# A hybrid decoder layer on one core: low-weight products last in each tile, columns normalised ahead of the input projection, a three-operation step in the top-k search

## The chip, the cores and the metric

The kernel runs on one core of a Trainium2 chip. The metric is the device time of one execution in microseconds. All times of the kernel before come from three runs and from one more execution that the hardware profiler recorded.

## The reference

One decoder layer for 1040 positions (16 meta tokens and 1024 of input) of 1024 channels:

```python
h = rms_norm(stream, mix_norm_g)
proj = h @ w_in          # conv branch, q/k/v, indexer q/k/weights, two gates
q, k, q_idx, k_idx = rope(...)
y_a = silu(layer_norm(conv31(a * sigmoid(gate)))) @ conv_pw_out
score = sum_h w_idx[h] * relu(q_idx[h] . k_idx)       # causal, meta keys first
keys  = top_k(score, 256)                             # per query
y_b = softmax(q . k[keys]) @ v[keys] @ attn_w_o
stream += (sigmoid(g_a) * y_a + sigmoid(g_b) * y_b) @ w_merge_out
h = rms_norm(stream, ffn_norm_g)
stream += (silu(a) * b) @ ffn_down                    # a, b = conv3(h @ ffn_up)
out = rms_norm(stream, final_norm_g)
```

`rms_norm` scales each position by the inverse root of its mean square, and each channel by a gain.

## The kernel before, in words

**Layout.** Channels lie on the 128 partitions and positions along the free axis, so an activation is eight tiles (`k` = 0 to 7) of 1044 columns. Column work is cut into three chunks of 348 (`CW`) or, without the first columns, of 342 (`QW`).

**Matrix products.** Every product is made of three in a 32-bit form that TensorE rounds: each operand is split into a high half (a rounded copy) and a low half (the rest). `mm` (L176) computes one tile of 128 output rows: for each `k` in turn it issues high weight by high data, high weight by low data, and low weight by high data, each for up to three chunks of columns. With eight `k` and three chunks that is 72 matmuls, each with its own weight load, into three banks of PSUM. `psm` (L203) alternates between two sets of three banks.

**Weights.** `wload` (L110) brings weight tile `i`: SP loads `wr`, ScalarE copies it to the high half `wh` (L117), writes its negative to `wl` (L121), and POOL issues a transfer that adds the weights from DRAM to it (L122), so that `wl` becomes the low half. The first two tiles take a VectorE subtraction instead (L119). There are three buffers of `wh` and two of `wl` and of `wr`; `wget` asks for a tile and the two behind it.

**The opening.** The input tiles `x` arrive chunk by chunk. Each is multiplied by its gain on the way into the high half `hh` (ScalarE, L274) and the low half `hl` (VectorE, L275). The squares (L284, L286) are added on POOL, or in the last chunk on VectorE (L288), summed over partitions by TensorE (`stat_mm`, L239, a column of ones as moving operand), turned into the inverse root `r` (`rstd_small`, L241), and spread over all partitions by TensorE (`bcast_mm`, L254) into `rx` (L295). The factor of the position comes in later, at each place where a projection is used: in the rope tables (L304), the values (through `rpos`, L335 and L340, which TensorE transposes from `rx`, L391), the indexer weights (L395), the convolution branch (L660 before its tanh and L673 on POOL), and the gates.

**Input projection.** The loop at L645 goes over units in a fixed list: convolution channel tiles, indexer keys and queries, gates, q, k and v. A gate tile is copied out of PSUM (L696) and stored to DRAM; `load_gate` (L762) fetches it during the projections `w_pw` and `w_o`, multiplies it by `rx` on POOL (L766) and takes its tanh on ScalarE (L767). Beside the units, `background` steps through the depthwise convolution taps (VectorE, L580) and the search for the top-k threshold.

**The search** (`topk_search`, L486) finds, for each query, the bits of the threshold from the highest down, for two groups of query blocks. For a bit ScalarE counts the scores at or above a candidate (L483). VectorE prepares the two candidates of the next bit (L503, L504), and behind the count compares (L507) and copies under the comparison to the next candidate (L509) and to `key` (L510).

**Behind it** come the projection `w_pw` (L796), attention over eight heads, the output projection `w_o`, the merge `w_merge`, and the feed-forward part in five groups (`w_up`, `w_down`).

**Order of work.** The program is written in this order, and a planner in the framework lays out each engine's own instruction list from it by simulated times and priorities; work under `urgent()` is moved ahead. On the chip every engine works through its list in order and waits on semaphores. SP and POOL issue transfers in the order of their lists too.

Of the kernel before, what the change touches and what calls it, by code (L numbers as in the profile page):

```python
# [11 lines left out]
F32 = mybir.dt.float32  # L12
# [65 lines left out]
def body(ctx: ExitStack, tc: tile.TileContext, xT, vecs, w_idx, w_v, w_conv, w_k, w_q, w_gate,  # L78
# [97 lines left out]
    def mm(ps, w, rh, rl, nk, cols, woff=0):  # L176
        wh, wl = w
        for k in range(nk):
            sl = slice(woff + k * P, woff + (k + 1) * P)
            for pi, (ww, rr) in enumerate(((wh, rh), (wh, rl), (wl, rh))):  # L180
                for ci, (c0, n) in enumerate(cols):
                    pe.matmul(ps[:, ci, :n], lhsT=ww[:, sl], rhs=rr[k][:, c0:c0 + n],  # L182
                              start=(k == 0 and pi == 0), stop=(k == nk - 1 and pi == 2))
# [49 lines left out]
    def vcol(i):  # L233
        return vec[:, i:i + 1]
# [25 lines left out]

# [5 lines left out]
    rx = ft("rx")  # L266
    rpos = base.tile([P, NB + 1], F32, name="rpos")
# [3 lines left out]
    for c in range(NCH):  # L271
        cs = slice(c * CW, (c + 1) * CW)
        for k in range(KT):
            act.activation(hh[k][:, cs], xs[k][:, cs], AF.Copy, scale=vcol(V_MG + k))  # L274
            dve.scalar_tensor_tensor(hl[k][:, cs], xs[k][:, cs], vcol(V_MG + k), f(hh[k])[:, cs], op0=ALU.mult,  # L275
                                     op1=ALU.subtract)
    acc = tmp("acc")
    for c in range(NCH):
        cs = slice(c * CW, (c + 1) * CW)
        for k in range(KT):  # L280
            sq = tmp(f"sq{c}_{k}") if k else None
            dst = sq[:, :CW] if k else acc[:, cs]
            if k % 2 and c < NCH - 1:
                dve.tensor_tensor(dst, xs[k][:, cs], xs[k][:, cs], op=ALU.mult)  # L284
            else:
                act.activation(dst, xs[k][:, cs], AF.Square)  # L286
# [3 lines left out]
    with urgent():  # L290
        r = rstd_small(PS[:, 6, :], BW, 9, "n1")
        for c in range(NCH):
            sb = bank("s", (7, 6))
            bcast_mm(sb, r, BW, 3 * c, 3)
            act.copy(rx[:, c * CW:(c + 1) * CW], sb[:, :CW])  # L295
    del xs
    d_rx = dram.tile([P, LQ], F32, name="drx")
# [15 lines left out]
    def values(ws):  # L313
# [10 lines left out]
        for b in range(NB + 1):  # L324
# [8 lines left out]
            with urgent():  # L333
                if b == 0:
                    act.activation(vm, ps[:M0, :VW], AF.Copy, scale=rpos[:M0, 0:1])  # L335
                else:
# [3 lines left out]
                    act.activation(vf[:, q * VW:(q + 1) * VW], ps[:, :VW], AF.Copy, scale=rpos[:, b:b + 1])  # L340
# [28 lines left out]
    def index_keys(w):  # L369
# [18 lines left out]
        sp_ = bank("s", (6, 7))  # L388
        for b in range(NB + 1):
            c0, m = (0, M0) if b == 0 else (M0 + P * (b - 1), P)  # L390
            pe.transpose(sp_[:m, b:b + 1], rx[0:1, c0:c0 + m], ident[:1, :1])  # L391
        act.copy(rpos[:M0, 0:1], sp_[:M0, 0:1])
        act.copy(rpos[:, 1:], sp_[:, 1:NB + 1])
        wqv = wq.rearrange("p j h -> p (j h)")[:, IH:]
        dve.scalar_tensor_tensor(wq[:, 1:, :], sb[:, IH:NB * IH].rearrange("p (j h) -> p j h", h=IH), IH ** -0.5,  # L395
                                 rpos[:, 2:].rearrange("p (j o) -> p j o", o=1).to_broadcast([P, NB - 1, IH]),
                                 op0=ALU.mult, op1=ALU.mult)
# [88 lines left out]
    def topk_search():  # L486
# [687 lines left out]
```

## Time and profile before

| | us |
|---|---|
| median of three runs | 1903.15 |
| lowest, highest | 1901.66, 1908.85 |
| the profiled execution | 1905.48 |
| its span, first to last instruction | 1903.7 |

The profiled execution lies 2.3 us above the median, and 1.8 us of it lie around its span. Its mean granted TensorE clock is 0.985 of full speed. Engines in the rows: PE is TensorE's matmuls, PEld its weight loads, DVE is VectorE, ACT ScalarE, POOL GpSimd, SP the engine that issues plain transfers; a `q` behind a name means its queue. A row names the line, the engine, the operation, the tile written and the tiles read; `<-` behind a time names what ended the wait. TensorE's matmuls overlap, so the mean of one is longer than the step from one to the next.

### The profile page before, as it was taken

To read this page: it belongs to the slowest core of one execution; us is meant where nothing else is said; L and a number is where in the kernel's file an instruction comes from. 1 tells how busy PE (TensorE), PEld (TensorE's weight loads), DVE (VectorE), ACT (ScalarE), POOL (GpSimd) and SP (SyncE) were. 2 spreads that over 40 slices of the span, in tenths; PEclk is the share of its full clock that TensorE was granted. 3 is DMA by queue.
4 is the path that set the end of the run, shared out by engine and by line. 5 is a ranking of instruction groups with operands and counts; after the bars stand their busy time and mean duration, and the time that the engine had idled before them with its cause. 6 is when DMAs were issued, how large, how long until landed. Compare 5 with 4: busy or idle time off the path is not lost.

```text
span 1903.7 us, 27576 instructions
## 1 busy us (share of the span) xinstructions
PE 1826.9 (96%) x11131; PEld 1755.1 (92%) x11131; DVE 1025.3 (54%) x1582; ACT 985.4 (52%) x1568; POOL 463.2 (24%) x395
## 2 busy tenths in 40 slices
PE   8889899999999989999999999999999999999997
PEld 7879799999999989899999999988998999899987
DVE  6597598998954392588833223331432233133436
ACT  6555477888799933688732334322332233233325
POOL 4533332122123235122221221111121111111122
PEclk9999999999999999999999999999999999999999
DMA  5533467777656588421267444444434443544342
GB/s 183 125 78 86 99 139 165 157 167 155 144 133 156 128 194 221 101 68 46 78 177 199 89 111 89 85 87 105 95 78 93 102 90 78 119 90 89 67 91 97
DMA packets 71696, 221.59 MB, mean 116 GB/s; under 512 B 7897, under 2 KB 17425, under 8 KB 71569
## 3 DMA queue, kind: packets, MB, share of 16 engines
q0 software_dynamic: 26208, 88.67, 26.5%
q1 hardware_dynamic: 45360, 131.16, 23.0%
q8 instruction: 87, 1.43, 0.3%
q14 instruction: 41, 0.33, 0.1%
HBM read 176.15 MB, written 23.68 MB: 105 GB/s over the span
## 4 chain that ended last, share of the span: by engine, by line
PE 44%; issue 12%; DMA 7%; ACT 4%; DVE 3%; POOL 3%; POOLq 0%; SPq 0%; DVEq 0%; ACTq 0%
PE PS L182 37%; PE PS L893 3%; PE PS L837 2%; ACT junk L483 2%; PE PS L871 1%; DMA wl<-w_up 1%; POOL wl L122 1%; DMA gate<-dth 1%; DMA wl<-w_o 1%; DMA wl<-w_pw 1%; DMA dza<-za 1%; DMA qld<-dq 1%; DVE ol L927 0%; ACT wl L121 0%; DMA wl<-w_gate 0%
## 5 line engine op out<-in xcount | busy, mean ns | idle before, releaser
L117 ACT CAST wh<-wr 128x1024 fp32r<-128x1024 f32 (+2 forms) x147 | 142.9, 972 | 451.2 <-PE PS L182 443.3
L182 PE MATMUL PS<-hh,wh 128*128 128x342 f32 (+2 forms) x1096 | 254.4, 328 | 17.7 <-DVE qx0t L356 5.4
L182 PE MATMUL PS<-hh,wl 128*128 128x342 f32 (+2 forms) x1096 | 254.6, 329 | 15.0 <-DMA wl<-w_conv 8.9
L182 PE MATMUL PS<-hl,wh 128*128 128x342 f32 (+2 forms) x1096 | 254.2, 329 | 2.9 <-DVE hl L275 2.7
L182 PE MATMUL PS<-h2h,wl 128*128 128x344 f32 x1056 | 224.4, 321 | 4.5 <-DMA wl<-w_up 4.5
L182 PE MATMUL PS<-h2l,wh 128*128 128x344 f32 x1056 | 225.1, 320 | 0.0
L182 PE MATMUL PS<-h2h,wh 128*128 128x344 f32 x1056 | 225.0, 320 | 0.0
L182 PEld LDWEIGHTS PS<-hh,wh 128*128 128x128 f32 x1096 | 191.0, 193 | 22.1 <-DVE qx0t L356 5.8
L182 PEld LDWEIGHTS PS<-hh,wl 128*128 128x128 f32 x1096 | 191.3, 192 | 19.2 <-DMA wl<-w_conv 10.3
L182 PEld LDWEIGHTS PS<-hl,wh 128*128 128x128 f32 x1096 | 191.2, 192 | 6.6 <-DVE hl L275 5.2
L483 ACT ACTIVATE junk<-sc,wn 128x1040 bf16<-128x1040 f32 (+6 forms) x217 | 182.4, 840 | 21.1 <-DVE key L510 16.6
L182 PEld LDWEIGHTS PS<-h2h,wl 128*128 128x128 f32 x1056 | 177.2, 189 | 5.4 <-DMA wl<-w_up 5.4
L182 PEld LDWEIGHTS PS<-h2h,wh 128*128 128x128 f32 x1056 | 178.1, 189 | 0.4
L182 PEld LDWEIGHTS PS<-h2l,wh 128*128 128x128 f32 x1056 | 177.8, 189 | 0.1
L580 DVE SCALAR_TENSOR_TENSOR cb<-g,dwh,cb 128x1026 f32<-128x1026 f32 x105 | 144.0, 1376 | 23.1 <-DMA cb<-ct 23.1
L580 DVE SCALAR_TENSOR_TENSOR co<-g,dwh,co 128x1026 f32<-128x1026 f32 x113 | 153.9, 1370 | 4.6 <-DMA co<-ct 4.5
L121 ACT ACTIVATE wl<-wr 128x1024 fp32r<-128x1024 f32 (+2 forms) x145 | 141.7, 977 | 5.7 <-PE PS L182 5.7
L1046 DVE TENSOR_TENSOR xr<-PS,xr 128x1024 f32<-128x1024 f32 x32 | 39.2, 1225 | 157.2 <-PE PS L182 157.2
L122 POOL DMA_DIRECT2D wl<-w_up x44 | 38.3, 871 | 300.4 <-ACT wl L121 287.9
L182 PE MATMUL PS<-uh,wl 128*128 128x512 f32 x304 | 95.6, 396 | 0.0
L182 PE MATMUL PS<-ul,wh 128*128 128x512 f32 x304 | 95.3, 395 | 0.0
L182 PE MATMUL PS<-uh,wh 128*128 128x512 f32 x304 | 95.3, 394 | 0.0
(590 smaller groups left out, 3531.0 us busy)
## 6 DMA issues: line engine op xcount, KB each, us to landing
wr<-w_up SPq DMA_DIRECT2D x44, 512.0 KB, 4.0
wl<-w_up POOLq DMA_DIRECT2D x44, 512.0 KB, 7.6
dth<-gt SPq DMA_DIRECT2D x16, 513.0 KB, 7.8
gate<-dth SPq DMA_DIRECT2D x16, 513.0 KB, 7.2
wr<-w_conv SPq DMA_DIRECT2D x16, 512.0 KB, 4.5
wr<-w_gate SPq DMA_DIRECT2D x16, 512.0 KB
wl<-w_gate POOLq DMA_DIRECT2D x16, 512.0 KB, 8.1
wr<-w_down SPq DMA_DIRECT2D x24, 320.0 KB, 3.0
```

Of the source, the lines that this page charges most:

```text
L117: act.copy(wh[:, :nk * P], raw[:, :nk * P])
L121: act.activation(wl[:, :nk * P], raw[:, :nk * P], AF.Copy, scale=-1.0)
L122: pool.dma_start(wl[:, :nk * P], src, accum_op=ALU.add)
L182: pe.matmul(ps[:, ci, :n], lhsT=ww[:, sl], rhs=rr[k][:, c0:c0 + n], start=(k == 0 and pi == 0), stop=(k == nk - 1 and pi == 2))
L483: act.activation(junk[:, :n], sc[j][:, PAD:PAD + n], AF.Sign, bias=bits.bitcast(F32)[:, slot[j]:slot[j] + 1], accum_out=cnt[:, slot[j]:slo ...
L580: dve.scalar_tensor_tensor(a, g[:, w:w + LQ], wt[w], a, op0=ALU.mult, op1=ALU.add)
L837: pe.matmul(lg[:, :nn], lhsT=qq[:, qc], rhs=kk[g][:, c0:c0 + nn], start=(pi == 0), stop=(pi == 2))
L871: pe.transpose(tp[:, b * P:(b + 1) * P], pts[e][:, c0:c0 + P], ident)
L893: pe.matmul(ov[:, q0:2 * P], lhsT=vv[g][:, vs], rhs=tt[kb // 4][:, rs_], start=False, stop=(kb == nkb - 1 and pi == 2))
L1046: dve.tensor_tensor(x, ps[:, :2, :], x, op=ALU.add)
```

## The change

It has three parts. In `mm` the three products change places with the loop over `k`: all `k` of high by high, then all of high by low, then all of low by high. In the opening each chunk's squares are summed over the eight tiles by TensorE at once, the inverse root is spread to PSUM, `x` is multiplied by gain and factor in place, and the halves are split from that; so `rx`, `rpos`, their transposes, their store and load, and all later multiplies go, and a gate's tanh is taken at its copy out of PSUM. In the search the comparison is turned round, shifted to the bit and combined with the candidate, so that `nxt` and `key` need no separate copies.

```diff
@@ mm @@
         wh, wl = w
-        for k in range(nk):
-            sl = slice(woff + k * P, woff + (k + 1) * P)
-            for pi, (ww, rr) in enumerate(((wh, rh), (wh, rl), (wl, rh))):
+        for pi, (ww, rr) in enumerate(((wh, rh), (wh, rl), (wl, rh))):
+            for k in range(nk):
+                sl = slice(woff + k * P, woff + (k + 1) * P)
                 for ci, (c0, n) in enumerate(cols):
                     pe.matmul(ps[:, ci, :n], lhsT=ww[:, sl], rhs=rr[k][:, c0:c0 + n],
                               start=(k == 0 and pi == 0), stop=(k == nk - 1 and pi == 2))
@@ the opening @@
     for c in range(NCH):
         cs = slice(c * CW, (c + 1) * CW)
+        sqs = []
         for k in range(KT):
-            act.activation(hh[k][:, cs], xs[k][:, cs], AF.Copy, scale=vcol(V_MG + k))
-            dve.scalar_tensor_tensor(hl[k][:, cs], xs[k][:, cs], vcol(V_MG + k), f(hh[k])[:, cs], op0=ALU.mult,
-                                     op1=ALU.subtract)
-    acc = tmp("acc")
...
+            if k % 3 == 0:
+                sqt = ft(f"sq{c}_{k}")
+            sq = sqt[:, (k % 3) * CW:(k % 3 + 1) * CW]
+            sqs.append(sq)
+            if k % 4 == 3:
+                dve.tensor_tensor(sq, xs[k][:, cs], xs[k][:, cs], op=ALU.mult)
+            else:
+                act.activation(sq, xs[k][:, cs], AF.Square)
+        sb = bank("s", (6, 7))
+        for b in range(3):
+            for k in range(KT):
+                pe.matmul(sb[:BW, b:b + 1], lhsT=sqs[k][:, b * BW:(b + 1) * BW], rhs=ones, start=(k == 0),
+                          stop=(k == KT - 1))
+        r = rstd_small(sb, BW, 3, f"n1{c}")
+        sb = bank("s", (6, 7))
+        bcast_mm(sb, r, BW, 0, 3)
         for k in range(KT):
...
-            if k:
-                (pool if c < NCH - 1 else dve).tensor_tensor(acc[:, cs], acc[:, cs], dst, op=ALU.add)
-    stat_mm(PS[:, 6, :], acc, 0, BW, 9)
...
-            act.copy(rx[:, c * CW:(c + 1) * CW], sb[:, :CW])
+            x = xs[k][:, cs]
+            dve.scalar_tensor_tensor(x, x, vcol(V_MG + k), sb[:, :CW], op0=ALU.mult, op1=ALU.mult)
+            act.copy(hh[k][:, cs], x)
+            (pool if k % 3 == 2 else dve).tensor_tensor(hl[k][:, cs], x, f(hh[k])[:, cs], op=ALU.subtract)
...
-    nc.sync.dma_start(d_rx, rx[:, Q0:LC])
...
-        pool.tensor_tensor(t[:, :LC], t[:, :LC], rx[:, :LC], op=ALU.mult)
@@ topk_search @@
                         dve.tensor_scalar(cand[:, s], cur[:, s], 1 << (b - 1), None, op0=ALU.bitwise_xor)
-                        dve.tensor_scalar(nxt[:, s], key[:, s], 1 << (b - 1), None, op0=ALU.bitwise_xor)
                 stat_counts(g, cur, b)
                 with urgent():
-                    dve.tensor_tensor(cond[:, s], cnt[:, s], kstat[:, s], op=ALU.is_ge)
-                    if b:
-                        dve.copy_predicated(nxt[:, s], cond[:, s], cand[:, s])
-                    dve.copy_predicated(key[:, s], cond[:, s], cur[:, s])
+                    dve.tensor_tensor(cond[:, s], cnt[:, s], kstat[:, s], op=ALU.is_lt)
+                    dve.scalar_tensor_tensor((nxt if b else key)[:, s], cond[:, s], b, (cand if b else cur)[:, s],
+                                             op0=ALU.logical_shift_left, op1=ALU.bitwise_xor)
@@ the units and the gates @@
-                dve.tensor_tensor(c3(th[:, :LC], CW), src, c3(rx[:, :LC], CW), op=ALU.mult)
-                act.activation(th[:, :LC], th[:, :LC], AF.Tanh, scale=0.5)
+                act.activation(c3(th[:, :LC], CW), ps[:, :, :CW], AF.Tanh, scale=0.5)
...
-                pool.tensor_tensor(g[:, GOFF:GOFF + LC], g[:, GOFF:GOFF + LC], rx[:, :LC], op=ALU.mult)
...
-                    act.copy(c3(th[:, :LQ], QW), ps[:, :, :QW])
+                    act.activation(c3(th[:, :LQ], QW), ps[:, :, :QW], AF.Tanh, scale=0.5)
...
-        pool.tensor_tensor(t[:, :LQ], t[:, :LQ], rq, op=ALU.mult)
-        act.activation(t[:, :LQ], t[:, :LQ], AF.Tanh, scale=0.5)
...
-    nc.sync.dma_start(rq, d_rx)
```

## Rows read from the trace of the kernel before

**Rows 1.** The page's first part: busy us (share of the span) and instructions of each engine.

```profile
PE 1826.9 (96%) x11131; PEld 1755.1 (92%) x11131; DVE 1025.3 (54%) x1582; ACT 985.4 (52%) x1568; POOL 463.2 (24%) x395
```

**Rows 2.** Waits of TensorE, whole span: line, awaited: us in total, times, longest.

```profile
PE PS L182 <- DMA wl<-w_pw: 9.4, 5, 4.8
PE PS L182 <- DMA wl<-w_conv: 8.9, 4, 3.6
...
PE PS L182 <- DMA wl<-w_o: 5.3, 2, 3.3
PE PS L182 <- DMA wl<-w_up: 4.5, 3, 1.8
PE PS L182 <- DMA wl<-w_gate: 3.6, 1, 3.6
PE PS L182 <- DVE th L660: 3.2, 1, 3.2
```

**Rows 3.** Timeline of TensorE, a dense tile: start, us, engine, line, operation, tiles, count.

```profile
1038.18 0.64 PE L182 MATMUL PS<-zh,wh 128*128 128x342 f32 x3
1038.66 0.64 PE L182 MATMUL PS<-zl,wh 128*128 128x342 f32 x3
1039.13 0.63 PE L182 MATMUL PS<-zh,wl 128*128 128x342 f32 x3
```

**Rows 4.** Stretches behind `wl` stalls, L182: length, PE busy (count), clock, DMA share, GB/s.

```profile
196.40:201.30 4.90, 4.90 (x17) 0.50 0.00 0
...
700.90:706.50 5.60, 5.60 (x20) 0.50 0.90 227
...
1025.20:1030.70 5.50, 5.50 (x19) 0.50 0.57 160
```

**Rows 5.** Timeline of POOL before 1025 us; in brackets the idle time before.

```profile
1009.81 2.39 POOL L766 TENSOR_TENSOR gate<-gate,rqb 128x1026 f32<-128x1026 f32 x1 [9.02 <-DMA gate<-dth]
```

**Rows 6.** Timeline of ScalarE, the same stretch.

```profile
1012.24 1.06 ACT L767 ACTIVATE gate<-gate 128x1026 f32<-128x1026 f32 x1 [10.57 <-POOL gate L766]
...
1014.14 1.05 ACT L121 ACTIVATE wl<-wr 128x1024 fp32r<-128x1024 f32 x1
```

**Rows 7.** DMA issues, whole span: count, KB each, median us from issue to landing.

```profile
x<-xT SPq DMA_DIRECT2D x24, 174.0 KB, 4.1
...
wl<-w_o POOLq DMA_DIRECT2D x8, 512.0 KB, 8.5
```

**Rows 8.** Timeline of VectorE behind the first output-projection tile.

```profile
950.25 1.22 DVE L944 SCALAR_TENSOR_TENSOR gate<-gate,PS 128x1026 f32<-128x1026 f32 x1 [1.96 <-PE PS L182]
...
953.86 1.23 DVE L948 TENSOR_TENSOR zl<-zar,zh 128x1026 fp32r<-128x1026 f32 x1 [1.12 <-ACT zh L947]
```

**Rows 9.** Timeline of SP at the start.

```profile
4.05 1.99 SPq L219 DMA_DIRECT2D x<-xT  x4
```

**Rows 10.** Timeline of TensorE, 37 to 59.5 us.

```profile
37.83 0.77 PE L239 MATMUL PS<-ones,acc 128*116 128x1 f32 x6 [0.67 <-DVE acc L288]
...
40.93 1.49 PE L256 MATMUL PS<-ident,n1r 116*128 116x116 f32 x12
44.97 1.24 PE L182 MATMUL PS<-hh,wl 128*128 128x348 f32 x3 [2.55 <-DMA wl<-w_idx]
...
58.53 0.64 PE L182 MATMUL PS<-hh,wl 128*128 128x348 f32 x3
```

**Rows 11.** Tile `x`: operation and count: ns least/median/most, first and last start.

```profile
L275 DVE SCALAR_TENSOR_TENSOR hl<-x,vec,hh x24: 568/572/1261, 8.8 to 33.0; 128x348 fp32r<-128x348 f32 x24
```

**Rows 12.** Groups of instructions by form: count | busy us, mean ns | idle before.

```profile
L275 DVE SCALAR_TENSOR_TENSOR hl<-x,vec,hh 128x348 fp32r<-128x348 f32 x24 | 19.9, 880 | 0.0
...
L288 POOL TENSOR_TENSOR acc<-acc,sq 128x348 f32<-128x348 f32 x14 | 16.9, 1207 | 10.9 <-DVE sq L284 10.3
```

**Rows 13.** Groups by line, the search's last copy.

```profile
L510 DVE COPY_PREDICATED key<-cond,wn 128x3 int32<-128x3 int32 (+1 forms) x62 | 9.7, 157 | 0.1
```

**Rows 14.** Busy us of all engines (PE, PEld, DVE, ACT, POOL) in one stretch.

```profile
225.00:500.00 275.00, 260.63 (x1625) 258.35 (x1623) 258.60 (x385) 216.64 (x369) 70.47 (x65) 0.99 0.72 156
```

More of the change, by code (lines that the diff above doesn't have):

```diff
@@ L265, in body @@
     hl = [ft(f"hl{k}", F32R) for k in range(KT)]
-    rx = ft("rx")
-    rpos = base.tile([P, NB + 1], F32, name="rpos")
     BW = CW // 3
@@ L272, in body @@
         cs = slice(c * CW, (c + 1) * CW)
+        sqs = []
         for k in range(KT):
-            act.activation(hh[k][:, cs], xs[k][:, cs], AF.Copy, scale=vcol(V_MG + k))
-            dve.scalar_tensor_tensor(hl[k][:, cs], xs[k][:, cs], vcol(V_MG + k), f(hh[k])[:, cs], op0=ALU.mult,
-                                     op1=ALU.subtract)
-    acc = tmp("acc")
-    for c in range(NCH):
-        cs = slice(c * CW, (c + 1) * CW)
-        for k in range(KT):
[L281 to L286, printed above, removed]
-            if k:
-                (pool if c < NCH - 1 else dve).tensor_tensor(acc[:, cs], acc[:, cs], dst, op=ALU.add)
-    stat_mm(PS[:, 6, :], acc, 0, BW, 9)
[L290 to L294, printed above, removed]
-            act.copy(rx[:, c * CW:(c + 1) * CW], sb[:, :CW])
+            if k % 3 == 0:
[14 more added lines that the diff above has]
+        bcast_mm(sb, r, BW, 0, 3)
+        for k in range(KT):
+            x = xs[k][:, cs]
+            dve.scalar_tensor_tensor(x, x, vcol(V_MG + k), sb[:, :CW], op0=ALU.mult, op1=ALU.mult)
+            act.copy(hh[k][:, cs], x)
+            (pool if k % 3 == 2 else dve).tensor_tensor(hl[k][:, cs], x, f(hh[k])[:, cs], op=ALU.subtract)
     del xs
-    d_rx = dram.tile([P, LQ], F32, name="drx")
-    nc.sync.dma_start(d_rx, rx[:, Q0:LC])
     def rope_table(name, src):
@@ L334, in values @@
                 if b == 0:
-                    act.activation(vm, ps[:M0, :VW], AF.Copy, scale=rpos[:M0, 0:1])
+                    act.copy(vm, ps[:M0, :VW])
                 else:
@@ L339, in values @@
                         vf = tmp(f"vf{b}")
-                    act.activation(vf[:, q * VW:(q + 1) * VW], ps[:, :VW], AF.Copy, scale=rpos[:, b:b + 1])
+                    act.copy(vf[:, q * VW:(q + 1) * VW], ps[:, :VW])
                     if q == 3:
@@ L387, in index_keys @@
             pe.transpose(sb[:, j * IH:(j + 1) * IH], wt[:IH, M0 + P * j:M0 + P * (j + 1)], ident[:IH, :IH])
[L388 to L393, printed above, removed]
         wqv = wq.rearrange("p j h -> p (j h)")[:, IH:]
-        dve.scalar_tensor_tensor(wq[:, 1:, :], sb[:, IH:NB * IH].rearrange("p (j h) -> p j h", h=IH), IH ** -0.5,
-                                 rpos[:, 2:].rearrange("p (j o) -> p j o", o=1).to_broadcast([P, NB - 1, IH]),
-                                 op0=ALU.mult, op1=ALU.mult)
+        dve.tensor_scalar(wqv, sb[:, IH:NB * IH], IH ** -0.5, None, op0=ALU.mult)
         dve.tensor_scalar(wx.rearrange("p j h -> p (j h)")[:, IH:], wqv, ID ** -0.5, None, op0=ALU.mult)
@@ L656, in body @@
             with urgent():
-                src = c3(th[:, :LC], CW) if i == 0 else ps[:, :, :CW]
-                if i == 0:
-                    act.copy(src, ps[:, :, :CW])
-                dve.tensor_tensor(c3(th[:, :LC], CW), src, c3(rx[:, :LC], CW), op=ALU.mult)
-                act.activation(th[:, :LC], th[:, :LC], AF.Tanh, scale=0.5)
+                act.activation(c3(th[:, :LC], CW), ps[:, :, :CW], AF.Tanh, scale=0.5)
             background(8, 1)
@@ L765, in load_gate @@
         nc.sync.dma_start(t[:, :LQ], d_th[i])
-        pool.tensor_tensor(t[:, :LQ], t[:, :LQ], rq, op=ALU.mult)
-        act.activation(t[:, :LQ], t[:, :LQ], AF.Tanh, scale=0.5)
         return t
-    rq = rx[:, Q0:LC]
     otiny = base.tile([P, NG * NH], F32, name="otiny")
@@ L806, in body @@
     del cout, sh, sl
-    rx = rq = None
     o_raw = [ft(f"o{h}") for h in range(NH)]
@@ L936, in body @@
     zh, zl = [], []
-    rq = ft("rqb")[:, :LQ]
-    nc.sync.dma_start(rq, d_rx)
     for m in range(KT):
@@ L951, in body @@
     del oh, ol
-    rx = rq = None
     x2, gh, gl = [], [], []
```

## The prediction

> **What bounds the kernel now.** The page's first part comes first: TensorE is busy for 96% of the span, every other compute engine for about half of it or less [rows 1]. So time is won only where TensorE stands still or runs slowly, and the waits of TensorE come next [rows 2]. The reader is to see that most of what it waits for has one form: `wl`, the low half of a weight tile, whose accumulating transfer has not landed. Five such groups sum to 9.4+8.9+5.3+4.5+3.6 = 31.7 us. A dense tile follows for scale: three matmuls take 0.47 to 0.48 us, 0.159 each, so the 72 of an ordinary tile take 11.5 us [rows 3]. The stretches behind the longer stalls are looked at for the granted clock: it is 0.50 there, the 1.2 GHz level, right after the engine had stood still, and 17 matmuls take 4.9 us [rows 4]. There are six such stretches (from 196.4, 310.5, 501.7, 700.9, 986.3 and 1025.2 us), together 97 matmuls in 26.3 us. At 0.159 they would take 15.4, so the clock adds 10.9 us to the stalls. Last, why one `wl` is late: POOL multiplies a gate tile at 1009.81, ScalarE takes its tanh at 1012.24 and only then reaches the negation that starts the next `wl`, at 1014.14 [rows 5, 6]; the transfer takes 8.5 us from its issue [rows 7].
>
> **Order of the products.** No matmul and no weight load is added, so dense tiles cost the same if a change of weights is free. Rows 3 show it: the step from `zh,wh` to `zl,wh`, which keeps the weights, is 0.48 us, that from `zl,wh` to `zh,wl`, which changes them, 0.47. What moves is the time at which `wl` is needed: from the third matmul group of the tile to two thirds of it, 48 x 0.159 = 7.6 us later. A `wl` buffer is still held to the end of its tile, so the next `wl` in it starts no later and no sooner than now; the longest single `wl` wait is 4.8 us [rows 2], under 7.6, so each stall should close, and with it the slow clock behind it: 31.7 + 10.9 = 42.6 us. I take half back for the projection that follows the convolution branch (`w_pw`): there the DMA engines are 0.90 busy [rows 4], and work pressed together may find them full. Its share is 9.4 us of stalls and 5.6 - 20 x 0.159 = 2.4 of clock, half of 11.8 is 5.9. **Term: -36.7 us**; its ends are -42.6 and, with the whole middle of the kernel paced by others (below), about -24.
>
> The price of the order is that a tile needs all eight columns of its moving operand in its first third, not one after the other. At the head of the merge stage, the last `zh` follows its tile by a VectorE op, another, and a ScalarE copy: from 950.25 to the subtraction at 953.86 that needs it, 3.6 us [rows 8]. TensorE has 7 x 3 matmuls to do before, 3.3 us: a stall of 0.3 us. At the head of the output projection the `oh` and `ol` come at VectorE's pace of 1.2 us each, as the `zl` of rows 8; behind the last `ol` there lie 27 matmuls instead of 9, 2.9 us more, but part of the earlier ones then lie ahead of it; I put 1.2 us. The up-projections' operand is one VectorE op shorter, and the down-projections have a whole up tile before them. **Term: +1.5 us**, from 0 to 5.
>
> **Normalising ahead.** Now the splits need no statistic. In future a chunk of 348 columns is squared, summed on TensorE, rooted, broadcast, multiplied, split. The last four tiles of chunk 0 are issued from 4.05 to 6.04 us, the last at about 5.6, and land 4.1 us later [rows 7, 9], at 9.7; square to 10.2. The sums are 24 small matmuls a chunk, two records each; six records take 0.77 us now, 0.13 each [rows 10]; the 32 of the second and third block can start only behind the last square, 4.1 us, to 14.3. From the end of the sums (38.60) to the broadcast (40.93) it takes 2.3 us now, and twelve broadcast records 1.49, six 0.75 [rows 10]: 17.4. Then VectorE does 8 multiplies and 6 subtractions a chunk. Such an op takes 0.57 us in the median and 0.88 in the mean of 24, beside 14 POOL adds, so a POOL op cost VectorE 24 x 0.31 / 14 = 0.53 [rows 11, 12]: 14 x 0.57 + 2 x 0.53 = 9.0, with about 1 for the next chunk's broadcast, 10.0 a chunk. The last low half is there at 17.4 + 29 = 46.4; behind it lie one pass of the gate tile and three of the other, 32 x 0.159 = 5.1, to 51.5; the indexer's key tile (11.5) ends at 63.0. Now it ends at 59.2, because a late `wl`, the half clock and the broadcasts stand in it from 40.93 to 51.1 [rows 10]; these go. **Term: +4 us.** Bounds: +0 if squares and splits overlap better; +23 if TensorE, which now has gaps, does the 144 matmuls at the lower clock, 0.29 each as in rows 4, instead of 0.159. I take the low end because now too TensorE is fed piece by piece there at the full clock most of the time.
>
> VectorE's multiplies read one operand from PSUM, its subtractions two from SBUF, and POOL's two subtractions a chunk read SBUF as well. The Trainium skill, SBUF — State Buffer, Who interferes with whom, says that a VectorE instruction with two SBUF inputs and a GpSimd instruction that reads SBUF exclude each other for the whole instruction. By that rule six POOL ops would cost up to 6 x 1.2 = 7.2 us rather than the 3.2 from rows 12, an estimate, and the opening would end 4 us later.
>
> **What falls away.** The `rx` multiply between PSUM and the first tanh goes, so PSUM is freed by ScalarE alone: the wait on `th` L660, 3.2 us [rows 2]. **Term: -3.2**, from 0 to -12 if other waits on VectorE shrink with it (POOL's multiplies by `rx` go too). A gate's tanh takes the place of the copy out of PSUM, one ScalarE op for one; its multiply and second tanh in the two projections go, which takes rows 5 and the first of rows 6 out of the chain to `wl`. That chain is counted already. On SP's queue one store and one load of `rx` go; on TensorE nine tiny transposes.
>
> **The search.** Three VectorE ops per bit and group replace five. The op that ScalarE needs is the second behind the count in both versions; the last copy (0.157 us, x62) [rows 13] lies behind it. A shift-and-xor may take 0.16 to 0.32. **Term: 0**: this runs beside a dense TensorE, and the masks are not needed before attention.
>
> **Sum.** -36.7 + 1.5 + 4 - 3.2 = -34.4; from the profiled 1905.5 us: 1871.1. The median of the runs shown lies 2.3 us below the profiled one, so 1869 us for a median.
>
> **Rivals.**
> - *Others pace the middle.* From 225 to 500 us VectorE is busy 258.6 of 275 us [rows 14], and TensorE hardly outruns it. Then the 8.9 + 3.6 us of `w_conv` and `w_gate` and their clock (11.7 us in 44 matmuls, 4.7 us more than at 0.159) do not come back: +17 minus some relief from the multiplies that go: 1869 + 13 = 1882. For: the number. Against: taps can be put off to 500 and later, and VectorE loses work.
> - *Serial opening (slower).* A chunk's broadcast is queued on TensorE behind all 48 matmuls of the chunk before, and these run at 0.29: 6.2 + 2.3 + 0.75 + 9.0 + 13.9 = 32.2 us a chunk, 97 for three, to 107 us where 51.5 was forecast: +55, 1924 us. It decides from some 45 us of extra opening. For: TensorE takes its queue in order. Against: squares and sums of later chunks need nothing of the earlier ones, and the order is planned by simulated time, which puts a ready broadcast ahead.
> - *Order without effect.* If a late `wl` follows whatever the tiles wait for (transfers that start when their tile ends and always miss the next), stalls only move to the last third: TensorE then loses what it lost, and the opening adds 4: 1903 + 4 - 3 = 1904. Against: 8.5 us of transfer and about 2 of issue stand against 11.5 + 7.6.
> - *Doesn't do what it says:* the planner may hoist other tiles' matmuls between the passes; that could only fill gaps (counted under other).
>
> **How the numbers follow.** A measurement of this kernel can tell about 0.5% from no change: under 1893.6 us is faster, over 1912.7 slower. Forecast 0.73, paced middle 0.13, no effect 0.07, serial opening 0.05, other 0.02. The forecast's own bounds go from 1869 - 5.9 - 1.5 - 8.8 = 1853 to 1869 + 19 + 3 = 1891, and the paced middle lies within. Range 1850 to 1891. Faster 0.87, same 0.07, slower 0.06.
>
> **What would show it.** Right: the five `wl` groups gone from TensorE's waits or under 5 us in sum; no half-clock stretches behind 310, 501, 986 and 1025; the indexer's key tile ending at 60 to 66 us; no rise of waits on `zh` or `oh` beyond 5 us. Wrong: `wl` still in the waits; first dense matmuls after 30 us, or the half clock up to 60 us; VectorE ops in TensorE's waits between 225 and 500 us in place of `wl`.

## The result, and the profile after

The changed kernel takes 1889.6 us in the median of four runs (1886.4 to 1891.7), the kernel before, run beside it, 1905.0 (1901.7 to 1908.9): ratio 0.9917, 95% interval 0.9891 to 0.9943. That is 15.5 us faster. The forecast of 1869 us lies 36 us below this median, and its sum was -34.4; the measured time is inside the range that was given, 1850 to 1891. The profiled execution took 1888.2 us, its span is 1886.4 where it was 1903.7. Its mean granted TensorE clock is 0.985, as before: what the order of the products gains in clock (0.990 when it stands alone, below), the opening and the head of attention lose.

The page's first part answers to [rows 1]: TensorE has 117 instructions more, VectorE and POOL have less to do.

```profile
PE 1834.7 (97%) x11248; PEld 1769.3 (94%) x11248; DVE 972.4 (52%) x1473; ACT 975.8 (52%) x1550; POOL 378.7 (20%) x359
```

TensorE's waits over the whole span answer to [rows 2] (line, what was awaited, us in total, times, longest):

```profile
PE PS L183 <- DVE qx0t L350: 4.8, 1, 4.8
PE PS L325 <- ACT wvh L314: 4.2, 1, 4.2
PE PS L812 <- DVE sm L813: 4.0, 2, 3.7
...
PE PS L183 <- ACT th L641: 3.3, 2, 2.1
...
PE PS L183 <- ACT hh L292: 2.3, 1, 2.3
```

No `wl` is left among them: all five groups of [rows 2], 31.7 us, are gone. The places that ran at the lower clock behind them do so no more. The windows behind 310, 501, 985 and 1025 us, where the kernel before stood at 0.50, the 1.2 GHz level (length, busy us and count of PE, PEld, DVE, ACT, POOL, then clock, DMA share, GB/s):

```profile
310.00:316.00 6.00, 6.00 (x39) 6.00 (x39) 3.36 (x4) 5.87 (x14) 0.74 (x1) 1.00 1.05 248
501.00:507.00 6.00, 6.00 (x40) 6.00 (x40) 6.00 (x10) 4.79 (x11) 0.00 (x0) 1.00 0.64 161
985.00:992.00 7.00, 7.00 (x46) 7.00 (x45) 3.33 (x3) 2.11 (x2) 0.86 (x1) 1.00 0.50 145
...
1025.00:1031.00 6.00, 6.00 (x40) 6.00 (x39) 1.23 (x1) 0.20 (x1) 0.00 (x0) 1.00 0.75 184
```

The stretch of [rows 14] shows the same: TensorE starts 1700 matmuls in it instead of 1625, and VectorE is busy for 243.5 us instead of 258.6.

```profile
225.00:500.00 275.00, 271.14 (x1700) 269.15 (x1699) 243.46 (x325) 235.71 (x411) 51.28 (x63) 1.00 0.75 165
```

So the part that was to win has won. The loss is in the opening. Its timeline of TensorE (start, us, engine, line, operation, tiles, count, in brackets the idle time before) answers to [rows 10]. A record is one instruction in the trace; each one-column 32-bit sum leaves two:

```profile
10.56 1.13 PE L284 MATMUL PS<-ones,sq 128*116 128x1 f32 x6 [1.89 <-ACT sq L280]
11.85 6.01 PE L284 MATMUL PS<-ones,sq 128*116 128x1 f32 x34 [0.16 <-DVE sq L278]
19.15 1.63 PE L257 MATMUL PS<-ident,n10r 116*128 116x116 f32 x6 [1.29 <-DVE n10r L252]
23.04 4.13 PE L183 MATMUL PS<-hh,wh 128*128 128x348 f32 x15 [2.26 <-ACT hh L292]
...
32.08 4.54 PE L284 MATMUL PS<-ones,sq 128*116 128x1 f32 x44
...
40.17 1.08 PE L284 MATMUL PS<-ones,sq 128*116 128x1 f32 x10
...
41.85 5.95 PE L284 MATMUL PS<-ones,sq 128*116 128x1 f32 x38
47.66 4.70 PE L183 MATMUL PS<-hh,wh 128*128 128x348 f32 x15
...
68.58 4.08 PE L183 MATMUL PS<-hh,wh 128*128 128x348 f32 x24 [2.07 <-ACT th L641]
...
76.32 3.99 PE L183 MATMUL PS<-hh,wl 128*128 128x348 f32 x24
80.15 3.40 PE L183 MATMUL PS<-hh,wh 128*128 128x448 f32 x16
```

The first product starts at 23.0 us, where dense matmuls began at 7.7 before. Long runs of one-column sums stand between the products of the second and third chunk. The key tile is the one from 68.58; it ends where the next begins, at 80.15, and before it ended at 59.2 [rows 10]. Three stretches of this opening have the lower clock:

```profile
12.70:26.30 13.60, 10.05 (x45) 9.69 (x45) 6.30 (x17) 4.95 (x12) 2.25 (x2) 0.50 0.77 269
26.30:36.60 10.30, 9.12 (x75) 8.83 (x74) 2.81 (x7) 3.98 (x11) 3.71 (x2) 1.00 0.00 0
36.60:40.00 3.40, 3.40 (x13) 3.40 (x13) 0.82 (x5) 0.21 (x1) 0.00 (x0) 0.50 0.52 157
40.00:43.40 3.40, 3.40 (x34) 3.40 (x34) 1.35 (x3) 0.73 (x2) 0.00 (x0) 1.00 0.03 5
43.40:53.60 10.20, 10.20 (x44) 10.20 (x44) 6.44 (x17) 3.33 (x8) 1.85 (x2) 0.50 0.00 1
```

Each of them sets in while TensorE does nothing but one-column sums, or just behind such a run. The last has no idle time ahead of it: TensorE was busy for all of the 6.8 us before, unlike in [rows 4]. Together they are 27.2 us.

The stages one by one, each from the first matmul of the one to that of the next, in us of the span (for the kernel before, the key tile's end is that of its last matmul, 59.2; the next tile starts at 59.7):

| stage | before | after | difference |
|---|---|---|---|
| to the end of the key tile | 59.2 | 80.15 | +20.9 |
| key tile to the first of `w_pw` | 610.5 | 587.8 | -22.7 |
| `w_pw` | 106.8 | 94.9 | -11.9 |
| attention | 158.9 | 166.2 | +7.3 |
| `w_o` | 102.8 | 92.4 | -10.4 |
| merge | 91.1 | 91.9 | +0.8 |
| feed-forward and end | 774.4 | 773.1 | -1.3 |
| span | 1903.7 | 1886.4 | -17.3 |

### The profile page after: what moved, and what is told of

Same layout as the page of the kernel before. It is cut to its first block, busy times and chain, and to the rows that moved or that the text cites. A ratio compares the mean times of both kernels' runs of the same rounds, so it can differ in the third digit from the quotient of the medians.

```text
span 1886.4 us, 27586 instructions
## 1 busy us (share of the span) xinstructions
PE 1834.7 (97%) x11248; PEld 1769.3 (94%) x11248; DVE 972.4 (52%) x1473; ACT 975.8 (52%) x1550; POOL 378.7 (20%) x359
## 4 chain that ended last, share of the span: by engine, by line
PE 85%; DVE 6%; ACT 3%; DMA 3%; issue 2%; POOL 1%; SPq 0%; POOLq 0%; DVEq 0%; ACTq 0%
PE PS L183 73%; PE PS L868 3%; PE PS L812 3%; PE PS L846 2%; PE PS L414 1%; PE PS L325 1%; DVE co L564 1%; DVE cb L564 1%; ACT junk L469 1%; DMA x<-xT 1%; PE PS L284 1%; DVE cum L524 1%; DMA cb<-ct 0%; DMA wvr<-w_v 0%; DMA dza<-za 0%
## 5 line engine op out<-in xcount | busy, mean ns | idle before, releaser
L183 PE MATMUL PS<-hh,wh 128*128 128x342 f32 (+2 forms) x1096 | 195.4, 332 | 14.5 <-DVE qx0t L350 4.8
L183 PE MATMUL PS<-hl,wh 128*128 128x342 f32 (+2 forms) x1096 | 190.8, 325 | 1.2 <-POOL hl L293 1.2
L183 PE MATMUL PS<-hh,wl 128*128 128x342 f32 (+2 forms) x1096 | 191.6, 327 | 0.0
L183 PEld LDWEIGHTS PS<-hl,wh 128*128 128x128 f32 x1096 | 178.8, 190 | 3.0 <-POOL hl L293 1.5
L183 PE MATMUL PS<-h2h,wh 128*128 128x344 f32 x1056 | 174.8, 320 | 1.2 <-DVE ua0u L975 0.7
L183 PE MATMUL PS<-h2l,wh 128*128 128x344 f32 x1056 | 174.5, 320 | 0.0
L183 PE MATMUL PS<-h2h,wl 128*128 128x344 f32 x1056 | 174.4, 320 | 0.0
L991 POOL TENSOR_TENSOR ul<-us,uh 128x1026 fp32r<-128x1026 f32 x22 | 53.7, 2439 | 122.9 <-ACT uh L990 120.4
L183 PE MATMUL PS<-ul,wh 128*128 128x512 f32 x304 | 77.0, 399 | 0.0
L183 PE MATMUL PS<-uh,wh 128*128 128x512 f32 x304 | 76.5, 397 | 0.0
```

The costliest lines, as they stand in the source:

```text
L991: pool.tensor_tensor(lo[:, :LQ], s[:, :LQ], f(hi)[:, :LQ], op=ALU.subtract)
```

## The experiments

Two theories stood at first. A: the order of the products brings all that was forecast of it and the opening takes about half of it back. Its rivals: others pace the middle of the kernel, so that the order alone brings less; or the opening is cheap, and the gain is lost in the stages behind it.

### The order of the products alone

The kernel before with this edit in `mm`, and nothing else:

```diff
-        for k in range(nk):
-            for pi, (ww, rr) in enumerate(((wh, rh), (wh, rl), (wl, rh))):
+        for pi, (ww, rr) in enumerate(((wh, rh), (wh, rl), (wl, rh))):
+            for k in range(nk):
```

> The kernel before with the new order of the three products alone. Theory A (the order alone takes every late low-weight tile out of TensorE's way; the opening of the change costs some 21 us and hides half of it): the five wl groups vanish from TensorE's waits (31.7 us) with the half clock behind them (10.9), some 3 to 9 us come back at heads of stages: 1863 to 1872 us. Rival B (the w_pw and w_o stalls were closed by the gate chain that leaves the two projections, not by the order): only w_conv, w_gate and w_up go, wl<-w_pw and wl<-w_o stay near 9 and 5 us: about 1887. Rival C (the middle is paced by VectorE): about 1890, with waits on VectorE in place of wl between 225 and 500 us.

Measured: 1871.8 us against 1900.7, ratio 0.984 (0.9821 to 0.9859). Theory A, at the upper end of its range. The medians differ by 28.9 us; between the two profiled executions the span falls by 33.3, where the prediction had 35.2 for the order and its boundaries. Of the 31.7 us of `wl` waits 0.7 are left, one wait on `w_conv`. So the rivals that let the order win little (others pace the middle, stalls that only move, or stalls that only the gates' change closes) fall. Not all of it went as the prediction has it, though. One new wait is large, in `w_pw`:

```profile
PE PS L183 <- DVE za L800: 6.2, 1, 6.2
```

VectorE's `za` behind a `w_pw` tile frees the PSUM banks that the next tile needs, and it needs a gate that POOL and ScalarE have still to finish. So `w_pw` takes 102.2 us here, against 106.8 before and 94.9 in the full change, where the gate comes finished from DRAM and this wait is gone.

### The normalising ahead alone

The changed kernel with the old loop in `mm`, and with the five operations of the search of before put back: opening, gates and rope as changed.

```diff
-        for pi, (ww, rr) in enumerate(((wh, rh), (wh, rl), (wl, rh))):
-            for k in range(nk):
+        for k in range(nk):
+            for pi, (ww, rr) in enumerate(((wh, rh), (wh, rl), (wl, rh))):
```

> The change without the new order and without the new search: columns normalised ahead, gates' tanh taken early. Theory A: the opening costs about 21 us to the end of the indexer's key tile (59.2 to 80), wl stalls on w_conv, w_gate and w_up stay (17 us and some clock), those on w_pw and w_o shrink only in part, th's wait of 3.2 us goes: 1908 to 1922. Rival B: w_pw and w_o stalls vanish with the gate chain (14.7 us and 6 of clock): about 1902. Nothing for the opening (my forecast of +4): 1890 or less.

Measured: 1909.9 us against 1900.7, ratio 1.0052 (1.0033 to 1.0071): slower than the kernel before. Theory A in the main. By itself this part costs some 9 us by the medians (4.5 between the two profiled spans), net of what it saves later. Where each kernel differs from the one before, in us of the span:

| stage | order alone | normalising alone | whole change |
|---|---|---|---|
| to the first of `w_pw` | -25.1 | +15.9 | -1.7 |
| `w_pw` | -4.6 | -7.1 | -11.9 |
| attention | +5.8 | +3.0 | +7.3 |
| `w_o` | -9.9 | -9.9 | -10.4 |
| merge | +1.6 | -0.3 | +0.8 |
| feed-forward and end | -1.1 | +2.9 | -1.3 |
| span | -33.3 | +4.5 | -17.3 |

One thing the first theory did not have, and its rival did: in `w_o` TensorE waits for nothing in either kernel (5.3 us for `wl` before). The order closes these stalls, and so do gates that come finished from DRAM; together they win no more there than each alone. The parts do not add elsewhere either: up to `w_pw` the two make -9.2, the whole change -1.7. Why the new opening costs more beside the new order, no run here asks.

### The new search alone

The kernel before with the three-operation step of the search, and nothing else.

```diff
                         dve.tensor_scalar(cand[:, s], cur[:, s], 1 << (b - 1), None, op0=ALU.bitwise_xor)
-                        dve.tensor_scalar(nxt[:, s], key[:, s], 1 << (b - 1), None, op0=ALU.bitwise_xor)
...
-                    dve.tensor_tensor(cond[:, s], cnt[:, s], kstat[:, s], op=ALU.is_ge)
-                    if b:
-                        dve.copy_predicated(nxt[:, s], cond[:, s], cand[:, s])
-                    dve.copy_predicated(key[:, s], cond[:, s], cur[:, s])
+                    dve.tensor_tensor(cond[:, s], cnt[:, s], kstat[:, s], op=ALU.is_lt)
+                    dve.scalar_tensor_tensor((nxt if b else key)[:, s], cond[:, s], b, (cand if b else cur)[:, s],
+                                             op0=ALU.logical_shift_left, op1=ALU.bitwise_xor)
```

> The kernel before with the three-operation search alone. Theory A: no change, 1905 within 4 us, because ScalarE waits for the second VectorE operation behind its count in both versions and TensorE does not wait for the search. Rival: VectorE is what paces 225 to 500 us, so the some 19 us less of VectorE work there show as 5 to 10 us less in time.

Measured: 1900.3 us against 1900.7, ratio 1.0001 (0.9981 to 1.0021). No effect, as forecast.

### Where the opening loses: the squares ahead

The prediction's opening is a chain of squares, sums, root, spreading, multiplies, splits. In this kernel, all under `urgent()`, all squares and all 72 sums of the three chunks come first, and the rest of the chunks follows, so that no chunk waits for its squares behind the splits of the one before.

```diff
     for c in range(NCH):
...
-        sb = bank("s", (6, 7))
         for b in range(3):
             for k in range(KT):
-                pe.matmul(sb[:BW, b:b + 1], lhsT=sqs[k][:, b * BW:(b + 1) * BW], rhs=ones, start=(k == 0),
+                pe.matmul(PS[:BW, 6, 3 * c + b:3 * c + b + 1], lhsT=sqs[8 * c + k][:, b * BW:(b + 1) * BW], rhs=ones,
...
-        r = rstd_small(sb, BW, 3, f"n1{c}")
-        sb = bank("s", (6, 7))
+    for c in range(NCH):
+        cs = slice(c * CW, (c + 1) * CW)
+        r = rstd_small(PS[:, 6, 3 * c:3 * c + 3], BW, 3, f"n1{c}")
+        sb = PS[:, 7, :]
```

> The changed kernel with the squares and sums of all three chunks put ahead of the first chunk's normalisation. Theory A1 (the opening is long because the squares of chunks 1 and 2 stand behind chunk 0's splits on ScalarE and VectorE, although their x has landed): the convolution's first tiles end near 55 instead of 66 us, time near 1879. Rival A2 (the 72 small sums on TensorE and its lower clock are the cost): the sums are still there, the first tiles end within 4 us of 66, time within 4 us of 1889.6.

Measured: 1890.6 us, ratio 0.9944 (0.9929 to 0.9959), as the changed kernel; the key tile ends at 81.4. So taking the squares ahead wins nothing: the sums are still there, now in one block. The timeline of TensorE, and the window of that block:

```profile
10.76 26.59 PE L284 MATMUL PS<-ones,sq 128*116 128x1 f32 x136 [1.83 <-ACT sq L281]
38.65 1.63 PE L257 MATMUL PS<-ident,n10r 116*128 116x116 f32 x6 [1.30 <-DVE n10r L252]
41.46 3.85 PE L183 MATMUL PS<-hh,wh 128*128 128x348 f32 x12 [1.18 <-ACT hh L294]
```

```profile
11.20:37.40 26.20, 26.15 (x134) 26.00 (x134) 3.10 (x8) 7.09 (x14) 0.00 (x0) 0.50 0.53 178
```

136 records (68 sums) take 26.59 us, 0.196 each, back to back, at a granted clock of 0.50 from 11.2 us on. In [rows 10] six of them took 0.13 each.

### Where the opening loses: the sums done twice

```diff
-        for b in range(3):
+        for b in (0, 1, 2, 0, 1, 2):
```

> The changed kernel with the 72 one-column sums of the opening done twice, the second time into the same place. Theory A (they stand on the path): 72 more at 0.26 (full clock) to 0.39 us (half clock) are 19 to 28 us, of which the first chunk's part may lie beside its squares, so +12 to +28: 1902 to 1918 us. Rival B (TensorE has slack in the opening): less than +4, 1887 to 1894 us.

Measured: 1916.8 us, ratio 1.0086 (1.0063 to 1.011). Theory A. Timeline of TensorE:

```profile
10.60 17.31 PE L284 MATMUL PS<-ones,sq 128*116 128x1 f32 x88 [1.65 <-ACT sq L280]
...
39.72 15.63 PE L284 MATMUL PS<-ones,sq 128*116 128x1 f32 x90
...
60.77 15.78 PE L284 MATMUL PS<-ones,sq 128*116 128x1 f32 x88
...
95.87 4.36 PE L183 MATMUL PS<-hh,wh 128*128 128x348 f32 x16 [2.07 <-ACT th L641]
```

The key tile starts at 95.87 instead of 68.58: 72 more sums cost 27.3 us, 0.379 each, all of it on the path. Nothing in the opening hides them.

### The sums as wide matmuls

Here the squares are the moving operand, 348 columns in the rounded 32-bit form, against a matrix of ones. Eight matmuls a chunk give the sum on all partitions at once. The refinement of the root is left out, and the spreading is not needed.

```diff
-        for b in range(3):
-            for k in range(KT):
-                pe.matmul(sb[:BW, b:b + 1], lhsT=sqs[k][:, b * BW:(b + 1) * BW], rhs=ones, start=(k == 0),
-                          stop=(k == KT - 1))
-        r = rstd_small(sb, BW, 3, f"n1{c}")
-        bcast_mm(sb, r, BW, 0, 3)
+        for k in range(KT):
+            pe.matmul(sm[:, :CW], lhsT=onesr, rhs=sqs[k], start=(k == 0), stop=(k == KT - 1))
+        act.activation(rt[:, :CW], sm[:, :CW], AF.Sqrt, scale=1.0 / D, bias=eps)
+        dve.reciprocal(sb[:, :CW], rt[:, :CW])
```

> The changed kernel, but a chunk's squares are summed by eight matmuls that take the squares as the moving operand (348 columns, rounded 32-bit form) against a matrix of ones, so that the sum arrives on all partitions and needs no spreading; the root is taken on 348 columns (one ScalarE op from PSUM, one VectorE reciprocal) and the refinement step of the root is left out. Theory A (the opening's some 21 us are the 72 one-column sums, 144 records at 0.13 to 0.196 us, with the low clock that goes with them): eight times 0.159 = 1.3 us a chunk take the place of 6 to 9 us and the clock rises earlier; the key tile ends at 63 to 67 us instead of 80, the time is 1872 to 1877 us. Rival B (the chunks are paced by VectorE and ScalarE or by how the planner lays out the order, and the sums are only what TensorE does meanwhile): the key tile ends behind 75 us, 1884 us or more.

Measured: 1873.5 us, ratio 0.9857 (0.9833 to 0.9881), 16 us under the changed kernel. Theory A, and with the times that its expectation had named. Timeline of TensorE:

```profile
27.15 1.55 PE L287 MATMUL PS<-sq,onesr 128*128 128x348 f32 x8
...
51.61 4.10 PE L183 MATMUL PS<-hh,wh 128*128 128x348 f32 x24 [2.07 <-ACT th L644]
...
63.19 3.41 PE L183 MATMUL PS<-hh,wh 128*128 128x448 f32 x16
```

Its opening has two stretches at the lower clock, 10.3 us in all, fewer than the 27.2 with one-column sums:

```profile
13.40:20.30 6.90, 3.96 (x14) 3.96 (x15) 6.86 (x11) 4.46 (x10) 1.87 (x2) 0.51 1.04 354
...
30.50:33.90 3.40, 3.26 (x11) 3.26 (x12) 3.40 (x8) 3.36 (x8) 1.72 (x2) 0.50 0.00 0
```

Eight wide sums take 1.55 us. The key tile ends at 63.2, where the prediction had 63.0 for one-column sums. The rest of the kernel is as in the changed one: the span is 16.9 us shorter, the start of the key tile 17.0 us earlier. So nearly the whole gap between forecast and result (17.1 us of span) is the way in which the sums are done, with the root and the spreading that go with it. Beside the order alone nothing is won or lost: the opening is still 6.3 us longer than there (56.9), `w_pw` 5.5 shorter (96.7 for 102.2).

### Does the clock or the number of sums cost it?

A 128-column matmul (a filler) behind the third and the sixth of each eight one-column sums. That makes 18, where the expectation counts 24:

```diff
                 pe.matmul(sb[:BW, b:b + 1], lhsT=sqs[k][:, b * BW:(b + 1) * BW], rhs=ones, start=(k == 0),
                           stop=(k == KT - 1))
+                if k % 3 == 2:
+                    pe.matmul(PS[:, c, :P], lhsT=ident, rhs=ident, start=True, stop=True)
```

> The changed kernel with one 128-column matmul (plain 32-bit, identity by identity, 0.37 us at the full clock) put in behind every third one-column sum of the opening: 24 of them, 8.8 us of additional work. If the low clock in the opening (12.7 to 26.3, 36.6 to 40 and 43.4 to 53.6 us, 27 us in all, 13.6 us lost) is the greater part of the cost and additional dense columns lift it: -5 us, 1882 to 1888 us, and fewer stretches at 0.50. If the number of small matmuls is the cost, or the fillers don't lift the clock: +5 to +15, 1895 to 1905 us.

Measured: 1893.3 us, ratio 0.9954 (0.9939 to 0.997): between the two expectations. Where the fillers lie (two records each; least, median and most ns, first and last start), the longest run of sums in the first chunk, and the windows of the opening at the lower clock:

```profile
L287 PE MATMUL PS<-ident x36: 275/275/561, 6.8 to 18.5; 128*128 128x128 f32 x36
```

```profile
12.22 3.89 PE L284 MATMUL PS<-ones,sq 128*116 128x1 f32 x34
```

```profile
15.20:28.90 13.70, 9.70 (x40) 9.42 (x40) 9.35 (x21) 6.45 (x16) 1.90 (x2) 0.50 0.60 205
...
35.70:56.20 20.50, 20.50 (x97) 20.50 (x97) 8.61 (x24) 4.26 (x10) 1.97 (x3) 0.50 0.09 27
```

All 18 fillers (0.22 us each at the full clock, where the expectation had 0.37) lie between 6.8 and 18.7 us, ahead of the first product; none stands between the sums of the second and third chunk, where the lower clock now lasts 20.5 us. In all it is 34.2 us at 0.50 instead of 27.2. So this run does not separate the two. In the first chunk, behind the first fillers, the 34 records took 3.9 us, nearly all at the full clock, where the changed kernel took 6.0 at the lower one; whether the fillers did that, one run does not show.

Other rows separate them in part. In the changed kernel the 44 records from 32.08 us on, at the full clock, step to the next matmul in 4.4 us, 0.10 each, against 0.196 at the lower. The 144 records more of the doubled sums cost 27.3 us, of which 14.4 would be their number at 0.10: an estimate by which about half of the price is their number and half the clock at which they run.

### Order and search without the new opening

If the opening costs and the order wins, the order with the search and the old opening should be the best of the parts: the kernel before with the edits of the first and the third experiment.

> The kernel before with the order of the products and the new search alone, old opening and old gates. Theory A (order is the whole gain, the opening takes some 17 us of it back, the search is worth nothing): as with the order alone, 1868 to 1874 us. Rival B (with TensorE no longer held by weights the search's shorter chain counts): below 1867 us.

Measured: 1883.1 us, ratio 0.9909 (0.9886 to 0.9933). Both expectations missed: 11 us slower than the order alone. In the traces, 10.1 us of span, 8.3 are lost between the key tile and `w_pw`, 4.3 in `w_pw`, and 2.5 are won behind it. From 205 to 660 us TensorE waits more, at many small places. First the order alone, then with the search:

```profile
PE PS L183 <- DVE th L661: 2.6, 1, 2.6
PE PS L332 <- ACT wvh L321: 2.1, 1, 2.1
...
PE PS L183 <- DVE kr1t L357: 0.3, 1, 0.3
```

```profile
PE PS L183 <- DVE th L659: 4.0, 2, 2.6
PE PS L183 <- DMA wl<-w_conv: 2.3, 3, 1.3
...
PE PS L183 <- DVE qr2t L357: 1.5, 1, 1.5
PE PS L183 <- DVE kr1t L357: 1.1, 1, 1.1
```

Three kernels ask whether the new search itself costs this. Two put the old search back, in the changed kernel and in the one with wide sums; one adds two idle VectorE operations per bit and group to the slow kernel, so that their number is the old one:

```diff
                         dve.tensor_scalar(cand[:, s], cur[:, s], 1 << (b - 1), None, op0=ALU.bitwise_xor)
+                        dve.tensor_scalar(spare[:, s], cst[:, NJ:2 * NJ][:, s], 1 << (b - 1), None, op0=ALU.bitwise_xor)
...
+                    dve.copy_predicated(spare[:, s], cond[:, s], cur[:, s])
```

> The changed kernel with the search of before (five VectorE operations a bit). If the new search costs the same here as beside the order alone (1883 against 1872): 11 us less than the changed kernel, 1876 to 1881 us. If that loss came from how the instructions happened to be laid out in that one kernel: no difference, 1887 to 1893 us.

Measured: 1890.1 us, ratio 0.9934 (0.991 to 0.9959): as the changed kernel. The search is worth nothing there.

> The kernel with wide sums (eight matmuls of 348 columns a chunk instead of 24 one-column sums) and the search of before. If the new search costs 11 us wherever the order is changed: 1861 to 1866 us, below the order alone and the fastest so far. If it costs nothing here: 1871 to 1877 us.

Measured: 1873.6 us, ratio 0.9842 (0.9815 to 0.9868): as with the new search. Worth nothing there either.

> Order of the products and new search, with two more VectorE operations per bit and group that go to a spare tile (one xor ahead of the count, one copy under the comparison behind it), so that the number of operations is that of the old search again. If the loss of 11 us beside the order alone is in how the planner lays out the other work around a shorter search: it goes, 1869 to 1875 us, though more is done. If it is in the new operations themselves (a slower step from the count to the next candidate): it stays, 1881 to 1888 us.

Measured: 1880.1 us, ratio 0.9886 (0.9862 to 0.991). More work, and no more time: 3 us less, which the intervals do not tell apart. Neither expectation is met; most of the loss stays. So the search costs nothing in three pairs (the kernel before, the changed kernel, wide sums) and 11 us in the fourth, where the old opening stands beside the new order. That pair alone still has VectorE's multiply by `rx` between PSUM and the tanh (`th`) together with a TensorE that is no longer held by weights. That this multiply makes the difference is a guess; no run here took it away by itself, and the cause stays open.

## Why the prediction was wrong

Of the four signs of being right that it named, three came: no `wl` in TensorE's waits, no half clock at the four places, no waits on `zh` or `oh`. The fourth, the key tile ending at 60 to 66 us, did not: it ends at 80.15.

**Order of the products: right in its mechanism, and in its sum partly by luck.** -36.7 and +1.5 were forecast; the order alone gave -33.3 of span, or 28.9 between the medians. The `wl` waits and the half clock behind them went, but the parts are off in both directions. From the key tile to `w_pw` 22.8 us were won where the terms had 17.2 (12.5 of waits, 4.7 of clock); in `w_o` 9.9 where they had 9.0 (5.3 and 3.7); in the feed-forward part 1.1 where they had 4.5, as small waits on `xr` and `wdh` came in the place of `wl`. Changing the weights cost nothing, as read from [rows 3]: a dense pass of 24 matmuls takes 3.8 to 3.9 us in the timeline after, 0.16 each. In `w_pw` half of 11.8 was taken back, 5.9 left, and the order alone won 4.6: near in size, wrong in its reason. The DMA engines were busy for 0.80 of that stage, not full; what was lost went to a gate that came late. With the gates finished ahead the stage won 11.9.

**The boundaries: more than their upper end.** +1.5 was forecast, at most +5. The merge stage is 0.8 us longer, but attention 7.3 (5.8 with the order alone). One wait was not foreseen, at its head. In the list of VectorE's waits of that stretch:

```profile
DVE p L813 <- DMA dza<-za: 4.4, 1, 4.4
```

VectorE's softmax step needs a buffer from which the last `za` of `w_pw` is still being stored, and TensorE waits behind it for `sm` (3.7 us) and then runs at a granted clock of 0.57 for 3.4 us. In the kernel before that wait of VectorE was 1.0 us. Timelines of SP there, first before, then after, and what SP's load waited for after:

```profile
777.99 0.32 SPq L801 DMA_DIRECT2D dza<-za  x1
```

```profile
765.56 0.33 SPq L113 DMA_DIRECT2D wr<-w_o  x1
765.99 0.38 SPq L777 DMA_DIRECT2D dza<-za  x1
```

```profile
SPq L113 <- ACT wl L121: 7.8, 1, 7.8
```

VectorE asks for the buffer 4.4 us behind the end of that `za` in both kernels. Before, the store went out at once, and the softmax step started 5.5 us behind `za`. After, the load of the next weight tile stands ahead of the store in SP's list and waits for ScalarE; the store goes out 1.7 us late, beside that load, and the softmax step starts 8.8 us behind `za`. With the order alone the load stands ahead too (wait of 3.7 us); with the normalising alone it does not (1.2 us). So the loss comes with the order, by way of the list that the planner made for SP: load first in the two kernels with the new order, store first in the two without it. A buffer of its own for that tile, or the store first, was not tried.

**What falls away: larger, and in another place.** -3.2 was forecast, for the wait on `th`, with -12 as the other bound. From the key tile to `w_pw` nothing came of it: that stage takes 587.7 us with the order alone and 587.8 in the whole change. The wait on `th` there fell from 2.6 to 1.2 us, but others grew (`wvh` from 2.1 to 4.2, `r` from 3.2 to 5.0). `w_pw` is 7.3 us shorter than with the order alone. The gates' multiply and second tanh, which the prediction took as counted with `wl`, are worth this where the order alone waits for `za`.

**The search: right by itself,** with the one pair above left open.

**Normalising ahead: the failed step.** +4 was forecast, +20.9 came. The prediction hid the sums of the second and third chunk behind VectorE; the runs show them on TensorE's path. The step went wrong in two places that its own rows allowed to be seen.
- The pace of a chunk was taken from VectorE alone, 10.0 us. TensorE's own work for a chunk was never added up: 48 matmuls by 0.159 and 48 records by 0.13 and 0.75 for the spreading are 14.6 us. TensorE was the bound of the opening: 72 more sums made it longer by all that they took. VectorE did its 14 operations of a chunk in 6.6 to 7.1 us.
- Of the sums only the first chunk's 4.1 us were put on the path. From 17.4 to 51.5 us, 34.1, were forecast for the three chunks' products, and they took from 20.8 to 66.5, 45.7. In these 45.7 us TensorE's timeline has 11.4 for the sums of the second and third chunk (4 and 44 records, 10 and 38: 0.3 + 4.4 + 0.9 + 5.8), 1.3 for two spreadings, 3.4 of waits, and 29.6 for the 144 products, 22.9 of it by 0.159 each and 6.7 that the lower clock adds. The first multiply was 3.4 us late (20.8 for 17.4): the first chunk's 34 records started at 11.9 instead of 10.2 and took 6.0 us instead of 4.1. The tanh that frees PSUM adds the 2.07 us wait ahead of the key tile. 11.6 + 3.4 + 2.1 = 17.1, and 80.15 - 63.0 = 17.2.

The low clock in the opening, put at the low end because TensorE was mostly at the full clock there before, was 27.2 us, against 10.3 with wide sums. That +20.9 lies near the +23 that was given as the other bound is chance: that bound took all 144 products at the lower clock and left the sums hidden. The "serial opening" that was given as the rival on the other side had this place and this mechanism, TensorE's queue, and set its price too high (32.2 us a chunk, where the first multiplies of the chunks came 21 and 14 us apart), as it took the lower clock for all matmuls.

**VectorE and POOL.** The prediction weighed 3.2 us for six POOL subtractions by [rows 12] against 7.2 by the rule that it cites from the Trainium skill, SBUF — State Buffer, Who interferes with whom. The runs show both engines held. On POOL (timeline, changed kernel) one of the six takes 4.92 us: beside it run ten VectorE operations, six subtractions and four squares, with both operands in SBUF, back to back from 24.72 to 29.12 us. The others take 0.93, the first of them beside VectorE multiplies with one operand in PSUM:

```profile
23.84 0.93 POOL L293 TENSOR_TENSOR hl<-x,hh 128x348 fp32r<-128x348 f32 x1 [20.86 <-ACT hh L292]
24.98 4.92 POOL L293 TENSOR_TENSOR hl<-x,hh 128x348 fp32r<-128x348 f32 x1 [0.21 <-ACT hh L292]
```

On VectorE six subtractions take 2.67 us in the first chunk and 3.15 and 3.17 in the others, 1.0 us more in all; the multiplies keep 0.57 throughout. The Trainium skill says there that a VectorE instruction with two SBUF inputs and a GpSimd instruction that reads SBUF contend for an exclusive lock, and the trace agrees. The price on VectorE was 1.0 us, and TensorE waited 1.2 us for the late half, so this was a small part of the +20.9.

## What to carry to other kernels

Where a change gives work to the engine that bounds the kernel, add up that engine's own work per step and compare it with the pace of the others before you say who sets the pace. Price a sum over partitions by how many matmuls it makes: 24 more matmuls of one moving column cost about 9 us a chunk here, and eight of 348 columns, which did the same sums, ran in 1.55. Test a change's parts alone as well as together: the order alone (1871.8 us) and the change with wide sums (1873.5) are both better than the whole change (1889.6), and cannot be told apart.

## What the runs showed of the hardware

TensorE's granted clock was 0.50, the 1.2 GHz level, through a block of one-column records without a gap (134 of them from 11.2 to 37.4 us, squares ahead), and in the changed kernel it fell during such sums at 43.4 us, after a stretch without idle time. Such a record steps in 0.10 us at the full clock and 0.196 at the lower. A one-column sum costs more than a matmul of 342 columns in the rounded form (two records by 0.10, against 0.159 at the full clock). A POOL subtraction that took 0.93 us beside VectorE multiplies with one operand in PSUM took 4.92 beside a run of ten VectorE operations with both operands in SBUF; the multiplies took 0.57 with POOL beside them and without.
